# A hybrid attention layer: TensorE's order in its linear attention written out as one woven sequence, and six mask steps placed around the fifth block

## The chip, the cores and the metric

The kernel runs on one core of a Trainium2 chip. The metric is the device time of one execution in microseconds (us). The engines are TensorE (PE, with PEld for its weight loads), VectorE (DVE), ScalarE (ACT), GpSimd (POOL) and SyncE (SP); each works through its own queue in order.

## What is computed

One decoder layer on 1024 tokens of width 1024. A joint projection `proj = rmsnorm(x) @ w_in` feeds two mixers. One is sparse attention, which keeps 256 keys per query, chosen by an indexer's scores. The other is gated linear attention with 4 heads, and it is here that the change lies:

```
log_a = log_sigmoid(g_lr @ gla_gate_w2 + gla_gate_b) / 16
# per chunk: b = cumsum(log_a)
attn[t,s] = sum_d q[t,d] k[s,d] exp(b[t,d] - b[s,d])    (s <= t)
o     = attn @ v + (q * exp(b)) @ state
state = exp(b_last) * state + (k * exp(b_last - b))^T @ v
o_b   = rmsnorm(o) * silu(r_gate)
```

Both outputs are projected and added to x, and a mixture of experts follows.

## The kernel before

The tokens are 8 tiles of 128. A projection of one tile is 24 matmuls of 128x384 (`project_steps`, L275; eight pieces of the depth, with high and low halves of the weights, wh and wl), collected in one of two PSUM banks `pj`. The linear attention has two pairs of heads p and, for each, four blocks u of two tiles: `gla2(0,0)` is the first block and `gla2(1,0)` the fifth of eight. Each pair has a set of projections for queries, keys and values (`project_qkv`, copied out on ACT, L405) and one for a second head's values and the output gates (`project_vr`: ACT L410 to L414, then the swish product gv on DVE, L415).

- `gla1(p,u)` prepares a block: transposes of q and k (L635, L636), for pair 0 of the gate's 16 rows too (L646, copied to glT on ACT), the gate matmul z (L651), then a chain on ACT, DVE and POOL (scans L665, L666; products L688 to L694) to the decayed operands dd.
- `gla2(p,u)` has four levels of eight small matmuls (L711) and a fifth with four (L715), each into two of three banks `mm`, from which DVE copies under a mask into `at` (L719, L724); transposes of kd; then for each tile the outputs (L741, L744) and the state (L748, DVE L752); then squares (ACT L758), a reciprocal root and o (DVE L764). It leaves `finish`, the transposes of o (L771) and their store, to be called later.
- `search` makes passes of bisection over the indexer's scores (DVE L528 on four or six tiles, ACT L521 on two), seven in all; `make_mask` builds the mask of one tile (POOL L587, DVE L589 to L595). Both are written between the blocks. After them a flag is made (PE L811, cast on DVE L813) and loaded, and an If (L815) guards a rare repair.

Up to the If a scheduler orders PE by the order in which the code is written and by its own costs (L779 to L805). Behind the If PE's order is written by hand: `weave` takes steps from a main generator and fills each step's stated time times ROOM with projections from a second one (`gla_main` and `gla_fill`: blocks five to eight with the last vr projections of pair 1 and the first attention projections).

## Time and profile before

| | before |
|---|---|
| median of 3 runs | 1082.19 us (1080.2 to 1083.65) |
| the profiled execution | 1076.3 us, span 1074.5 us |
| mean granted clock of TensorE | 0.965 |
| PE, DVE, ACT, POOL busy | 990.3, 764.2, 674.0, 382.2 us |

The linear attention's blocks lie between about 110 and 350 us of the span; the times in the rows below count from its start. Busy time says how full an engine is, not what it waits for; that is in the waits and in the timeline, where the idle time before an instruction and what ended it stand in brackets. The granted clock is the share of full speed that TensorE was given in a stretch.

### The profile page before, as it was taken

How to read it: one execution, taken by the hardware profiler on the slowest of the kernel's cores; microseconds unless marked ns; L12 is line 12 of the kernel's file. 1: busy time of each engine (PE TensorE's matmuls, PEld its weight loads, DVE VectorE, ACT ScalarE, POOL GpSimd, SP SyncE). 2: the span in 40 equal slices, each digit the busy share in tenths (PEclk: the TensorE clock that was granted, in tenths of full speed). 3: DMA queues.
4: the chain of work that ended last, by engine and by line, in shares of the span. 5: the costliest groups of instructions: out<-in, count | busy, mean ns of one | idle time of the engine just before them, and what ended most of it. 6: DMA issues, size and time to landing. Idle time of an engine off the chain costs nothing.

```text
span 1074.5 us, 17967 instructions
## 1 busy us (share of the span) xinstructions
PE 990.3 (92%) x5839; PEld 803.9 (75%) x5839; DVE 764.2 (71%) x2037; ACT 674.0 (63%) x1662; POOL 382.2 (36%) x499
## 2 busy tenths in 40 slices
PE   7799989999998999999989999949999999999892
PEld 7789878878887988988977878836666666666561
DVE  6877898684775566767765666656887778888771
ACT  7688755365555666666755533427777777777660
POOL 4510325551413225245332201254435444443421
PEclk9899989999999999999999999968999999999996
DMA  8220202020202102012131379769999999999983
GB/s 251 81 60 1 60 1 70 11 70 21 70 11 70 38 9 65 10 51 79 58 93 48 126 255 381 292 223 286 318 317 320 326 327 324 333 316 324 341 281 46
DMA packets 83206, 170.88 MB, mean 159 GB/s; under 512 B 14856, under 2 KB 45760, under 8 KB 82976
## 3 DMA queue, kind: packets, MB, share of 16 engines
q1 hardware_dynamic: 75936, 148.01, 40.8%
q0 software_dynamic: 7168, 21.65, 9.4%
q8 instruction: 48, 0.79, 0.3%
q14 instruction: 54, 0.44, 0.1%
HBM read 148.23 MB, written 26.88 MB: 163 GB/s over the span
## 4 chain that ended last, share of the span: by engine, by line
PE 59%; DMA 14%; DVE 14%; ACT 7%; issue 3%; POOL 2%; SPq 1%; POOLq 0%; ACTq 0%; DVEq 0%
PE pj L275 19%; DMA out_dram<-y,idx 10%; PE pj L1138 8%; PE mm L1512 3%; PE po L964 3%; PE pj L1463 3%; PE pj L1464 3%; PE pj L1465 3%; PE tp L952 2%; DVE w L1386 2%; PE mm L1159 1%; PE mm L936 1%; PE tp L1473 1%; PE mm L711 1%; PE mm L935 1%
## 5 line engine op out<-in xcount | busy, mean ns | idle before, releaser
L275 PE MATMUL pj<-wh,w 128*128 128x384 f32 (+1 forms) x1152 | 322.9, 347 | 6.0 <-DVE gv L415 5.0
L275 PEld LDWEIGHTS pj<-wh,w 128*128 128x128 f32 x1152 | 211.4, 193 | 13.8 <-DVE gv L415 5.6
L1385 ACT ACTIVATE w<-w 128x512 fp32r<-128x512 f32 x320 | 192.0, 628 | 46.0 <-PE mm L1465 27.5
L1386 DVE TENSOR_TENSOR w<-w,w 128x512 fp32r<-128x512 f32 x283 | 187.2, 698 | 31.7 <-ACT w L1385 28.3
L275 PE MATMUL pj<-wl,w 128*128 128x384 f32 (+1 forms) x576 | 199.3, 346 | 1.5 <-POOL wl L263 1.1
L275 PEld LDWEIGHTS pj<-wl,w 128*128 128x128 f32 x576 | 111.8, 194 | 4.7 <-POOL wl L263 1.3
L1463 PE MATMUL pj<-w,xT 128*96 128x512 f32 x256 | 105.5, 412 | 0.6 <-ACT w L1385 0.5
L1464 PE MATMUL pj<-w,xT 128*96 128x512 f32 x256 | 101.9, 398 | 2.3 <-DVE w L1386 1.2
L1465 PE MATMUL pj<-w,xT 128*96 128x512 f32 x256 | 101.7, 397 | 0.0
L1138 PE MATMUL pj<-w,mhl 128*128 128x512 f32 x384 | 101.1, 404 | 0.0
L929 POOL TENSOR_TENSOR cb<-bt,maskb 128x256 f32<-128x256 f32 (+1 forms) x64 | 43.5, 682 | 122.1 <-DVE mx L940 103.4
L1537 POOL DMA_INDIRECT out_dram<-y,idx x30 | 52.4, 1748 | 90.0 <-ACT w L1385 53.6
L263 POOL TENSOR_TENSOR wl<-wr,wh 128x384 fp32r<-128x384 f32 x58 | 59.9, 1053 | 68.3 <-ACT wh L262 67.5
L1138 PEld LDWEIGHTS pj<-w,mhl 128*128 128x128 f32 x384 | 69.4, 189 | 12.8 <-DVE mhl L1130 0.4
L1386 POOL TENSOR_TENSOR w<-w,w 128x512 fp32r<-128x512 f32 x37 | 50.5, 1364 | 46.9 <-ACT w L1385 45.6
L1512 PE MATMUL mm<-w,hT 128*96 128x512 f32 x128 | 65.4, 592 | 0.5 <-ACT hT L1502 0.5
L943 ACT ACTIVATE z<-z,mx 128x128 f32<-128x128 f32 (+7 forms) x64 | 49.5, 774 | 22.4 <-DVE mx L940 22.0
L1463 PEld LDWEIGHTS pj<-w,xT 128*96 128x96 f32 x256 | 44.2, 173 | 15.1 <-ACT w L1385 1.3
L1465 PEld LDWEIGHTS pj<-w,xT 128*96 128x96 f32 x256 | 41.8, 163 | 18.0 <-DVE xT L1477 0.2
L1464 PEld LDWEIGHTS pj<-w,xT 128*96 128x96 f32 x256 | 41.8, 163 | 17.9 <-DVE w L1386 2.7
L1473 PEld LDWEIGHTS tp<-cf,xg 96*128 96x128 f32 x256 | 40.9, 209 | 15.8 <-issue 9.3
L1463 PE MATMUL mm<-w,hTt 128*96 128x512 f32 x64 | 50.8, 794 | 0.0
(379 smaller groups left out, 2151.7 us busy)
## 6 DMA issues: line engine op xcount, KB each, us to landing
w<-in_w_exp_gate_dram SPq DMA_DIRECT2D x64, 512.0 KB, 7.7
w<-in_w_exp_up_dram SPq DMA_DIRECT2D x64, 512.0 KB, 7.7
w<-in_w_exp_down_dram SPq DMA_DIRECT2D x64, 512.0 KB, 7.7
wr<-in_w_in_dram SPq DMA_DIRECT2D x80, 128.0 KB, 2.5
xt<-in_x_dram SPq DMA_DIRECT2D x16, 512.0 KB, 4.7
mt<-mixd SPq DMA_DIRECT2D x8, 512.0 KB, 4.3
out_dram<-xt SPq DMA_DIRECT2D x8, 512.0 KB, 3.6
h2d<-h SPq DMA_DIRECT2D x7, 528.0 KB, 5.8
```

Of the source, the lines that this page charges most:

```text
L263: (V if by[kk + k] == "V" else G).tensor_tensor(b, raw[:, k], f32(a), op=OP.subtract)
L275: T.matmul(ps[:, :width], x_, y_[k], start=(k == 0 and i == 0), stop=(k == KC - 1 and i == 2))
L943: A.activation(z[:, :L], z[:, :L], AF.Exp, bias=mn, scale=-1.0, accum_out=sums[:, i:i + 1])
L1138: T.matmul(ps, lhs[:, k % 4], w[k, c], start=(k == 0 and i == 0), stop=(k == KC - 1 and i == 2))
L1385: A.activation(a, u, AF.Copy)
L1386: (G if engine == "G" else V).tensor_tensor(b, u, f32(a), op=OP.subtract)
L1463: T.matmul(ps, x[0], y[0], start=first, stop=False)
L1464: T.matmul(ps, x[0], y[1], start=False, stop=False)
L1465: T.matmul(ps, x[1], y[0], start=False, stop=last)
L1473: T.transpose(tp[:, k, :n], x["xg"][:n, :D].rearrange("n (a p k) -> n a k p", a=2, k=4)[:, hf, k], ident[:n, :n])
L1512: T.matmul(pd[:n], hT0, parts[2 * hf], start=True, stop=False)
L1537: G.indirect_dma_start(out=out[0], out_offset=bass.IndirectOffsetOnAxis(ap=idx[:CAP, e:e + 1], axis=0), in_=y[:CAP], in_offset=None, compu ...
```

## The change

The order of PE up to the If is now written out by hand too. Two generators are woven: `first_pair` (`gla1`, `gla2`, searches and masks in their order) and `first_fill` (the vr projections of pair 0, which were issued ahead of the linear attention, then all projections of pair 1). A step that is not ready yields 0, which ends the filling for that step; the first tile of a set counts double. The fifth block and all vr projections of pair 1 now lie ahead of the If, masks 2 to 4 are written before the fifth block and 5 to 7 after it. Behind the If `gla1(1,2)` starts the main generator, which before began with a lead of 4000 ns for the filling. The last block's `finish` is called after one more step of filling and ahead of the rest of it. A block's `finish` is now called in the next block whatever its pair. The tile gq of q, k and v is split in two (gq and gw), so that v can be kept for longer (11 buffers), with two copies out of PSUM in the place of one.

```diff
@@ -72,8 +72,11 @@
 SPLIT_AT = (0, 0, 0, 0, 0, 0, 0, 1)
 OPAT = (0, 3)
 SHARE = (None, (1, 1, 1, 1, 1, 1, 0.85, 1.3), (1, 1, 1, 1, 1, 1, 0.85, 1.3), (1, 1, 1, 1, 1, 1, 1, 1.3))
-ROOM = (2.2, 2.8, 3.15, 3.3)
+ROOM = (3, 2.4, 2.4, 2.4)
+LEAD = (10000, 10000)
 OROOM = (0, 0, 0, 6000, 6000, 6000, 6000, 6000, 0)
+ROOM0 = (4, 4, 4, 4)
+MORE = 3
 LOG_FLOOR = -21.0 * 16.0
 LEVELS = (64, 32, 16, 8)
 BUCKET_START = [0, 1, 2, 3, 4, 5, 6, 7, 8, 9, 10, 11, 12, 13, 14, 15, 16, 19, 21, 24, 27, 31, 35, 40, 46, 52, 59,
@@ -237,7 +240,7 @@
     wp = p_h.enter_context(tc.tile_pool(name="wp", bufs=WBUFS, side="right"))
     hT = []
     p2 = ExitStack()
-    gqp = p2.enter_context(tc.tile_pool(name="gqp", bufs=10, side="right"))
+    gqp = p2.enter_context(tc.tile_pool(name="gqp", bufs=1, side="right"))
 
     p1 = ExitStack()
     scp = p1.enter_context(tc.tile_pool(name="scp", bufs=1, side="left"))
@@ -390,7 +393,7 @@
                         base=0, channel_multiplier=1)
 
 
-    gq, gv, pools = {}, {}, {}
+    gq, gw, gv, pools = {}, {}, {}, {}
 
     def qkv_load(p):
         c = p * P
@@ -401,8 +404,11 @@
         return load_w([(VB + 2 * c + P, P), (RG + 2 * c, 2 * P)], by=BY_VR[p])
 
     def evac_qkv(p, t, pj):
-        gq[p, t] = gqp.tile([P, 384], F32, name="gq", tag="gq", bufs=9)
-        A.activation(gq[p, t], pj[:, :384], AF.Copy, scale=rstd[:, t:t + 1])
+
+        gq[p, t] = gqp.tile([P, 256], F32, name="gq", tag="gq", bufs=NT)
+        gw[p, t] = gqp.tile([P, P], F32, name="gw", tag="gw", bufs=NT + MORE)
+        A.activation(gq[p, t], pj[:, :256], AF.Copy, scale=rstd[:, t:t + 1])
+        A.activation(gw[p, t], pj[:, 256:384], AF.Copy, scale=rstd[:, t:t + 1])
 
     def evac_vr(p, t, pj):
         g = pools["gvp"].tile([P, 384], F32, name="gv", tag="gv", bufs=NT)
@@ -458,6 +464,7 @@
                 index_operands(NT - 1)
                 yield 1000, NT - 1
         w = vr_load(0)
+        yield 0, "v"
         for t in range(NT):
             for ns in project_steps(t, w, lambda ps: evac_vr(0, t, ps)):
                 yield ns, 0
@@ -481,7 +488,7 @@
             score_sums(t)
             if t == 3:
                 relative_bias()
-        for _ in fill:
+        while next(fill)[1] != "v":
             pass
 
     p1b.close()
@@ -622,7 +629,7 @@
             room += ns
             while room > 0:
                 ns = next(fill, None)
-                if ns is None:
+                if not ns:
                     room = 0
                     break
                 room -= ns
@@ -723,8 +730,8 @@
                 else:
                     V.copy_predicated(a[:, h], gm[:, lv, None, :].to_broadcast([P, 2, P]), pav[h])
             yield 500
-            if lv == 1 and p in gla_out:
-                gla_out.pop(p)()
+            if lv == 1 and gla_out:
+                gla_out.popitem()[1]()
             if lv == 2:
                 tk = ps_tp()
                 for i in range(2):
@@ -736,7 +743,7 @@
         po = [ps[:, :2 * P].rearrange("p (i t) -> p i t", i=2) for ps in (ps_po(), ps_mm())]
         s = st_s[p]
         for i, t in enumerate(ts):
-            vals = (gq[p, t][:, 2 * P:], gv[p, t][:, :P])
+            vals = (gw[p, t], gv[p, t][:, :P])
             for h in range(2):
                 T.matmul(po[h][:, i], a[:, h, i], vals[h], start=True, stop=(t == 0))
             for h in range(2):
@@ -776,33 +783,59 @@
 
         gla_out[p] = finish
 
-    run(gla1(0, 0))
-    search(0)
-    search(1)
-    w = qkv_load(1)
-    run(gla1(0, 1))
-    for u in range(4):
-        run(gla2(0, u))
-        project_qkv(1, 2 * u, w)
-        project_qkv(1, 2 * u + 1, w)
-        if u < 2:
-            search(2 * u + 2)
-            search(2 * u + 3)
-            run(gla1(0, u + 2))
-        elif u == 2:
-            search(6)
-            search_end()
-            run(gla1(1, 0))
-    gla_out.pop(0)()
-    run(gla1(1, 1))
-    make_mask(2)
-    make_mask(3)
-    make_mask(4)
-    w = vr_load(1)
-    for t in range(4):
-        project_vr(1, t, w)
-    for t in range(5, NT):
-        make_mask(t)
+    ended = [0, 0]
+
+    def first_pair():
+        yield from gla1(0, 0)
+        yield LEAD[0]
+        search(0)
+        search(1)
+        yield from gla1(0, 1)
+        yield LEAD[1]
+        ended[1] = 2
+        for u in range(4):
+            for ns in gla2(0, u):
+                yield ns * ROOM0[u]
+            ended[0] = u + 1
+            if u < 2:
+                search(2 * u + 2)
+                search(2 * u + 3)
+                yield from gla1(0, u + 2)
+                ended[1] = u + 3
+            elif u == 2:
+                search(6)
+                search_end()
+                yield from gla1(1, 0)
+        yield from gla1(1, 1)
+        for t in range(2, 5):
+            make_mask(t)
+        for ns in gla2(1, 0):
+            yield ns * ROOM[0]
+        for t in range(5, NT):
+            make_mask(t)
+
+    def first_fill():
+
+        for ns, _ in fill0:
+            yield ns
+        w = qkv_load(1)
+        for t in range(NT):
+            while t >= MORE and ended[0] <= (t - MORE) // 2 or ended[1] <= t // 2:
+                yield 0
+            for ns in project_steps(t, w, lambda ps: evac_qkv(1, t, ps)):
+                yield ns if t else 2 * ns
+        w = vr_load(1)
+        for t in range(NT):
+            while ended[0] <= t // 2:
+                yield 0
+            for ns in project_steps(t, w, lambda ps: evac_vr(1, t, ps)):
+                yield ns if t else 2 * ns
+
+    fill0 = fill
+    with tc.manual_schedule(engines={mybir.EngineType.PE}):
+        fill = first_fill()
+        weave(first_pair(), fill)
+        run(fill)
 
 
     nb16 = const.tile([P, 1], F16, name="nb16")
@@ -893,26 +926,22 @@
                     attention_operands(*list(qk2s)[0])
                     yield 440
 
-    def gla_fill(w):
-        for t in range(4, NT):
-            yield from project_steps(t, w, lambda ps: evac_vr(1, t, ps))
-        load_bias(0, ap1)
-        yield from attention_projections(0)
-
     def gla_main():
-        yield 4000
-        for u in range(4):
+        yield from gla1(1, 2)
+        for u in range(1, 4):
             for ns in gla2(1, u):
                 yield ns * ROOM[u]
-            if u < 2:
-                yield from gla1(1, u + 2)
+            if u == 1:
+                yield from gla1(1, 3)
+        yield 5000
 
     manual = ExitStack()
     manual.enter_context(tc.manual_schedule(engines={mybir.EngineType.PE}))
-    fill = gla_fill(w)
+    load_bias(0, ap1)
+    fill = attention_projections(0)
     weave(gla_main(), fill)
+    gla_out.pop(1)()
     run(fill)
-    gla_out.pop(1)()
     p2.close()
     ap2 = p_att.enter_context(tc.tile_pool(name="ap2", bufs=1, side="left"))
     kT[1] = ap2.tile([P, 2, S], F32R, name="kT1")
```

DVE's queue under the search, before. A row is line, operation, tile written and tiles read; numbers behind names are buffers. gv_1638 is the swish product of the third tile, L719 the copies of the first level, L528 (jb) a part of a search pass, L684 and L692 operands of block (0,1).

```order
L551 TENSOR_TENSOR st_den_1814<-st_clo_1811,st_chi_1812 128x6
L553 TENSOR_TENSOR st_w_1815<-st_hi_1810,st_lo_1809 128x6
L684 COPY el_2041<-eb_2039 128x2
L415 SCALAR_TENSOR_TENSOR gv_1638<-pj_1613,rstd_70,gv_1638 128x256
L552 RECIPROCAL st_den_1814<-st_den_1814 128x6
L692 TENSOR_TENSOR eb_2039<-qk_2003,eb_2039 128x256
L554 TENSOR_TENSOR st_w_1815<-st_w_1815,st_den_1814 128x6
L719 COPY_PREDICATED at0_1841<-gm_105,mm_2055 128x2x64
L719 COPY_PREDICATED at0_1841<-gm_105,mm_2056 128x2x64
L555 SCALAR_TENSOR_TENSOR st_num_1813<-st_clo_1811,st_w_1815 128x6
L719 COPY_PREDICATED at0_1841<-gm_105,mm_2063 128x4x32
L556 TENSOR_TENSOR st_v_1807<-st_lo_1809,st_num_1813 128x6
L528 TENSOR_SCALAR jb_2217,st_c_1808<-maskb_108,st_v_1807 128x384
```

The same place now (line numbers are those of the changed file: gv L421, the pass L535, the products of block (0,0) L695 to L700); gv_1864 is the third tile's gv.

```order
L535 TENSOR_SCALAR jb_2199,st_c_1576<-maskb_108,st_v_1575 128x384
L535 TENSOR_SCALAR jb_2201,st_c_1576<-maskb_108,st_v_1575 128x512
L695 TENSOR_TENSOR dd_1646<-qk_1618,dd_1646 128x2x64
L696 TENSOR_TENSOR dd_1646<-qk_1618,dd_1646 128x2x64
L695 TENSOR_TENSOR dd_1646<-qk_1618,dd_1646 128x4x32
L696 TENSOR_TENSOR dd_1646<-qk_1618,dd_1646 128x4x32
L695 TENSOR_TENSOR dd_1646<-qk_1618,dd_1646 128x8x16
L696 TENSOR_TENSOR dd_1646<-qk_1618,dd_1646 128x8x16
L700 TENSOR_TENSOR dd_1646<-qk_1618,dd_1646 128x256
L535 TENSOR_SCALAR jb_2203,st_c_1576<-maskb_108,st_v_1575 128x640
L535 TENSOR_SCALAR jb_2205,st_c_1576<-maskb_108,st_v_1575 128x768
L421 SCALAR_TENSOR_TENSOR gv_1864<-pj_1732,rstd_70,gv_1864 128x256
```

The third tile's gv moved from ahead of a pass to behind it, and the copies of the first level from ahead of this pass to behind the next one.

PE around the flag, before (L811 is the flag, L646 the transposes of the gate's rows, L275 a projection, L651 the gate matmul, L711 a level):

```order
L811 LDWEIGHTS nb_3227
L811 MATMUL pj<-ch,nb_3227 1x1
L646 MATMUL tp<-cf,glr 16x128 x2
L275 MATMUL pj<-wh,w_323 128x384
L815 UNCONDITIONAL_BRANCH
L275 MATMUL pj<-wl,w_323 128x384
L275 MATMUL pj<-wh,w_323 128x384 x2
...
L651 MATMUL tp<-glT,w_106 128x256
L275 MATMUL pj<-wh,w_323 128x384
L275 MATMUL pj<-wh,w_356 128x384
L711 MATMUL mm<-dd 128x64 x4
```

And now (L844 the flag, L278 a projection, L718 a level):

```order
L278 MATMUL pj<-wh,w_423 128x384
L844 LDWEIGHTS nb_3465
L844 MATMUL pj<-ch,nb_3465 1x1
L278 MATMUL pj<-wh,w_133 128x384
L848 UNCONDITIONAL_BRANCH
L718 MATMUL mm<-dd 128x64 x4
L278 MATMUL pj<-wl,w_133 128x384
...
L278 MATMUL pj<-wl,w_133 128x384
L718 MATMUL mm<-dd 128x64 x4
```

Where 23 projections stood between the flag and the next block's levels, one stands there, and seven between the first two levels.

PE at the end of the last block, before (L744 the outputs, L861 the transposes of an attention tile, L771 the block's output, L935 the first scores of the attention); between L861 and L771 stand 15 projections:

```order
L744 MATMUL po<-st_s_1840,eb 128x128
L744 MATMUL mm<-st_s_1840,eb 128x128
L861 MATMUL tp<-cf,qk_4510 128x128 x4
L275 MATMUL pj<-wh,w_422 128x384
...
L275 MATMUL pj<-wh,w_423 128x384
L771 MATMUL tp<-cf,o 128x128 x4
L935 MATMUL mm<-kT_3644,qp 128x128
L936 MATMUL mm<-kT_3644,qp 128x128
```

And now (L751, L894, L778 and L964); 24 projections stand ahead of the attention's transposes and 9 behind:

```order
L751 MATMUL po<-st_s_1608,eb 128x128
L751 MATMUL mm<-st_s_1608,eb 128x128
L278 MATMUL pj<-wh,w_389 128x384
...
L278 MATMUL pj<-wh,w_423 128x384
L894 MATMUL tp<-cf,qk_4561 128x128 x4
L278 MATMUL pj<-wh,w_422 128x384
...
L278 MATMUL pj<-wh,w_423 128x384
L778 MATMUL tp<-cf,o 128x128 x4
L278 MATMUL pj<-wh,w_422 128x384
...
L278 MATMUL pj<-wh,w_423 128x384
L964 MATMUL mm<-kT_3882,qp 128x128
```

The output's transposes have 33 projections between them and the last outputs, where they had 15, and six more now stand behind them.

## Rows read from the trace of the kernel before

**Rows 1.** The page's first part (busy us, share of the span and instructions of each engine) and, of its fourth part, the chain that ended last by engine.

```profile
PE 990.3 (92%) x5839; PEld 803.9 (75%) x5839; DVE 764.2 (71%) x2037; ACT 674.0 (63%) x1662; POOL 382.2 (36%) x499
...
PE 59%; DMA 14%; DVE 14%; ACT 7%; issue 3%; POOL 2%; SPq 1%; POOLq 0%; ACTq 0%; DVEq 0%
```

**Rows 2.** Busy time by engine in the one stretch from 90 to 370 us: its length, then PE, PEld (weight loads), DVE, ACT and POOL with the number of instructions, the granted clock as a share of full speed, DMA share and GB/s.

```profile
90.00:370.00 280.00, 264.23 (x1665) 234.50 (x1664) 202.81 (x631) 164.39 (x438) 99.80 (x153) 0.97 0.15 40
```

**Rows 3.** PE's waits from 100 to 360 us: who waited for what, total us, how many times, the longest.

```profile
PE pj L275 <- DVE gv L415: 5.0, 2, 2.6
PE tp L771 <- DVE o L764: 4.9, 1, 4.9
PE mm L711 <- DVE dd L689: 2.1, 1, 2.1
PE po L741 <- DVE at L724: 1.9, 2, 1.3
PE pj L275 <- POOL wl L263: 1.1, 1, 1.1
```

**Rows 4.** Busy time by engine from 130 to 170 us, 10 us to a row, with the columns of rows 2.

```profile
130.00:140.00 10.00, 7.85 (x50) 7.31 (x48) 9.93 (x32) 7.05 (x15) 4.83 (x12) 1.00 0.00 1
140.00:150.00 10.00, 7.41 (x35) 7.07 (x35) 9.96 (x36) 5.36 (x10) 3.72 (x7) 0.66 0.01 2
150.00:160.00 10.00, 10.00 (x66) 9.36 (x64) 9.63 (x45) 5.46 (x14) 0.00 (x0) 1.00 0.00 0
160.00:170.00 10.00, 10.00 (x66) 9.06 (x65) 10.00 (x27) 6.20 (x14) 7.15 (x8) 1.00 0.48 120
```

**Rows 5.** Busy time by engine in the stretches behind the waits that end at 142.6, 218 and 346.6 us, with the same columns (the granted clock is the figure ahead of the DMA share).

```profile
142.60:146.40 3.80, 3.79 (x12) 3.79 (x13) 3.76 (x15) 2.59 (x4) 0.00 (x0) 0.50 0.01 4
...
218.00:220.00 2.00, 2.00 (x10) 1.66 (x9) 1.72 (x4) 2.00 (x4) 0.00 (x0) 0.61 0.00 0
220.00:222.00 2.00, 2.00 (x8) 2.00 (x8) 1.93 (x3) 1.95 (x3) 0.82 (x2) 0.54 0.00 0
...
346.60:349.00 2.40, 2.37 (x10) 2.23 (x11) 1.75 (x7) 0.76 (x2) 0.00 (x0) 0.50 0.49 119
349.00:351.50 2.50, 2.50 (x10) 2.40 (x9) 0.00 (x0) 0.00 (x0) 0.00 (x0) 0.50 0.31 105
```

**Rows 6.** The chain that ended last, in order of time: start, us, what ran.

```profile
142.61 6.32 PE pj L275 x24
...
154.74 4.17 PE pj L275 x24
```

**Rows 7.** ACT's timeline near 121 us: start, us, engine, line, operation, tile written and tiles read with their shapes.

```profile
120.87 0.34 ACT L410 ACTIVATE gv<-pj,rstd 128x128 f32<-128x128 f32 x1
```

**Rows 8.** ACT's timeline, one pair of search passes.

```profile
121.86 1.04 ACT L521 ACTIVATE ja<-maskb,st_v 128x896 bf16<-128x896 bf16 x1
...
123.21 1.13 ACT L521 ACTIVATE ja<-maskb,st_v 128x1024 bf16<-128x1024 bf16 x1
```

**Rows 9.** DVE's timeline: the two scans of a block, gv of the third tile, and the four sums of one search pass.

```profile
135.03 0.74 DVE L665 TENSOR_TENSOR_SCAN b<-zb 128x128 f32<-128x128 f32 x2
...
135.73 0.90 DVE L666 TENSOR_TENSOR_SCAN bc<-l 128x128 f32<-128x128 f32 x2
...
142.09 0.47 DVE L415 SCALAR_TENSOR_TENSOR gv<-pj,rstd,gv 128x256 f32<-128x256 f32 x1
...
143.81 0.61 DVE L528 TENSOR_SCALAR_CACHE_REDUCE jb<-maskb,st_v 128x384 bf16<-128x384 bf16 x1
...
144.68 0.74 DVE L528 TENSOR_SCALAR_CACHE_REDUCE jb<-maskb,st_v 128x512 bf16<-128x512 bf16 x1
...
145.75 0.87 DVE L528 TENSOR_SCALAR_CACHE_REDUCE jb<-maskb,st_v 128x640 bf16<-128x640 bf16 x1
...
146.54 1.01 DVE L528 TENSOR_SCALAR_CACHE_REDUCE jb<-maskb,st_v 128x768 bf16<-128x768 bf16 x1
```

**Rows 10.** PE's timeline around the flag (its one matmul, and the first level of a block behind it), and DVE's (the flag's cast, and the next operation with the idle time before it and what ended that).

```profile
254.34 0.16 PE L811 MATMUL pj<-ch,nb 128*1 128x1 f16 x1
...
260.10 0.66 PE L711 MATMUL mm<-dd 64*128 64x64 f32 x8
...
254.54 0.15 DVE L813 CAST flag<-pj 1x1 int32<-1x1 f32 x1 [2.98 <-PE pj L811]
258.80 0.48 DVE L415 SCALAR_TENSOR_TENSOR gv<-pj,rstd,gv 128x256 f32<-128x256 f32 x1 [4.11 <-DVEq L815]
```

**Rows 11.** PE's timeline behind the If: the projection that waited for a weight half.

```profile
290.01 0.45 PE L275 MATMUL pj<-wl,w 128*128 128x384 f32 x1 [1.13 <-POOL wl L263]
```

**Rows 12.** The last block's output: ACT's timeline (the first square of its outputs, and two weight copies with the wait before them), DVE's (the last o) and PE's (the output's transposes).

```profile
338.54 0.28 ACT L758 ACTIVATE gsq<-po 128x128 f32<-128x128 f32 x1
...
342.07 0.94 ACT L262 ACTIVATE wh<-wr 128x384 fp32r<-128x384 f32 x2 [0.59 <-DMA wr<-in_w_in_dram]
...
346.92 0.34 DVE L764 SCALAR_TENSOR_TENSOR o<-mm,ms,gv 128x128 f32<-128x128 f32 x1
...
346.63 1.16 PE L771 MATMUL tp<-cf,o 128*128 128x128 f32 x4 [4.93 <-DVE o L764]
```

## The prediction

> **What bounds the kernel now.** I read the busy times first, then the chain that ended last, then TensorE's waits, then the clock, and last the queues of the engines that TensorE waits for. TensorE (PE) is busy for 990.3 of the 1074.5 us, VectorE (DVE) for 764.2, ScalarE (ACT) for 674.0, and PE holds 59% of the chain [rows 1]. So the change is worth what it takes from PE's idle time, or adds to it. All that it moves runs between 100 and 350 us. There PE is busy for 264.23 of 280 us [rows 2], so 15.8 us are idle, and the waits name who ends them: DVE's swish gate gv (L415) 5.0 us in two waits, DVE's output o (L764) 4.9 us in one, DVE's decay operands dd (L689) 2.1, DVE's scores at (L724) 1.9, GpSimd's weight halves (L263) 1.1 [rows 3]. DVE stands behind nearly all of it, and from 130 to 170 us it is busy for 9.63 to 10.00 us of every 10 [rows 4]: there the search passes (L528) lie in the same queue as everything that PE waits for. [...] The chain shows the price: 24 projection matmuls take 4.17 us at full clock and 6.32 us behind the wait that ends at 142.61 [rows 6]. Busy time times what the clock lacks of 1 gives the loss: 3.79 x 0.50 = 1.9 us at 142.6, 2.00 x 0.39 + 2.00 x 0.46 = 1.7 at 218, 2.37 x 0.50 + 2.50 x 0.50 = 2.4 at 346.6, 6 us in all [rows 5]. So the most that any order of PE could win here is 15.8 + 6 = 22 us, or 2%. One projection matmul is 4.17 / 24 = 0.174 us; I use that price below.
>
> **What it changes nothing in.** The copy out of PSUM is split in two (gq and gw), which adds 16 instructions on ACT; the nearest row, a 128-wide copy from the same bank, is 0.34 us [rows 7], so 16 x 0.34 = 5.4 us are added to an engine that is 63% busy and ends none of the five waits above. I cost it at nothing; if ACT had no room, the swish gates behind it would come late, and these 5.4 us are the bound. The matmuls themselves are the same in number and shape. So the sum has four terms, all of them waits.
>
> **Term 1, the blocks of the first pair, up to the fifth block.** Before, the projections of values and gates (vr) for pair 0 were run between the first two transposes and the first levels, where the scheduler put them; now they are shared out among these, and 61 of them (10.6 us) stand between z of block (0,1) and the first level. That takes away the wait of the levels for dd, 2.1 us, and, as gv of tile 0 now stands ahead of the scans in DVE's queue, the first of the two waits for gv, about 2.4 us [rows 3]. Gone: 4.5 us. What is late next is read off DVE's and ACT's queues. (a) z of block (0,1) needs a copy on ACT that can come behind a pair of search passes of 1.04 and 1.13 us [rows 8]: 0 to 2.4 us with their read-outs. (b) gv of tile 2 now stands behind one search pass more, 0.61 + 0.74 + 0.87 + 1.01 = 3.2 us, but ahead of the scans of the next block, 0.74 + 0.90 = 1.6 us, which came before it at 142.09 [rows 9]: 0 to 1.6 us. (c) The levels' copies into at now stand behind a pass each. A level has 12 or 13 projections (2.1 to 2.3 us) behind it, the pass takes 3.2: 0 to 1.0 us in each of two levels. (d) At the end of block (0,2) no projection may be run, since the next tile of q, k would overwrite operands (the generator yields 0 until the block has ended). There the outputs wait for at as in the two waits of 1.9 us before [rows 3], now with no cover: 0 to 1.3 us more for each of two tiles. The new waits add up to between 0 and 8.6 us. DVE is full here, so I take two thirds, 5.7, and the term is 5.7 - 4.5 = +1.2 us. Whether the half-clock stretch behind 142.6 goes, stays or is doubled is worth 2.15 us either way [rows 6]; I leave it as it is. Ends: -6.6 and +6.3.
>
> **Term 2, the If.** The flag (L811) is a matmul on PE, its cast is on DVE, and DVE then loads it and branches. Before, the flag ran at 254.34, the cast at 254.54, and DVE's next operation started only at 258.80, after 4.11 us of its own queue [rows 10]. PE did not care: glr's transposes and 23 projections stood behind the flag. Now the flag is followed by one projection, the first level of block (1,1), seven projections, and the next level, and that one needs a PSUM bank that DVE frees only after the branch. PE has work for 0.17 + 0.66 + 1.22 = 2.1 us (a level's eight matmuls take 0.66 [rows 10]). DVE is back 258.80 - 254.34 = 4.46 us behind the flag, and then has one product and one copy to do, neither of them larger than the gv of 0.48 us in the same rows; at 0.4 each PE goes on after 5.2 us: 3.1 us idle, which is cover that was there before and is gone. Some of DVE's other work (the first operands of block (1,1)) is late by the same, and a half-clock stretch as behind the other three waits may follow: I add 1.1 us for both. Term: +4.2 us; ends +1 (DVE's return hidden under a late arrival of PE) and +6. [...]
>
> **Term 3, blocks six to eight.** These are run with the attention projections as filling, 56 of these to a block where there were 66, so the levels stand closer together. Of the five waits only the 1.1 us for GpSimd, at 290.01, lies between 255 and 341 us [rows 11]. Ends 0 and +2.5 (one more wait for at of 1.3 us in two of three blocks); I take +0.5.
>
> **Term 4, the last block's output.** Before, its transposes (L771) stood behind the attention transposes and 15 projections, and then PE waited 4.93 us for o. The chain between is on ACT and DVE: the squares start at 338.54, ACT then stood 0.59 us at a weight DMA and copied two weight tiles, and the last o starts at 346.92, while the transposes begin at 346.63 with the first ones [rows 12], so it takes 8.1 us up to the first transpose. Now 33 projections (5.7 us) stand there, 18 more, with the same attention transposes. If the chain stays as slow, 8.1 - 5.7 = 2.4 us of idle is left; without the weight copies in its way, none. I take 1.0. The half clock behind it, 2.4 us, goes with the long idle. Term: -(4.93 - 1.0) - 2.4 = -6.3; ends -7.3 and -2.5 (2.4 us idle left and the clock as before).
>
> **Sum.** 1.2 + 4.2 + 0.5 - 6.3 = -0.4 us. It is made against the profiled execution, 1076.3 us (span 1074.5). The median of the runs shown is 1082.19, with 1080.2 to 1083.65 around it; the difference carries over, so I forecast 1081.8 us, which is no difference: a measurement of this kernel tells about 0.3% (3.2 us) from no change.
>
> **The rivals.** Faster: the sharing-out really covers. Term 1 loses the 4.5 us and gets half of the new waits (4.3), DVE's return is partly under PE's arrival (term 2 +1), and term 4 gives all of its 7.3 us, -0.2 + 1 - 7.3 = -6.5, and with the half-clock stretch at 142.6 gone too -8.6: 1073.6 to 1075.7 us. For it speaks that one idle of 4.93 us and its clock are nearly half of all that is to be had and that its cover is plainly longer now; against it, that DVE has no idle time in 130 to 170 us to give. Slower: the If decides. DVE's 4.11 us now lie on PE's path, and if PE arrives at the flag with nothing queued but eight projections, all of 6 us are paid; the first blocks pay their 6.3 as well if DVE reaches each level behind a search pass, and term 4 returns only 5. 6 + 6.3 + 1 - 5 = +8.3: up to 1090.5 us, and from 3.2 us of term 1 on it is slower to be measured. For it speaks the full DVE [rows 4], against it that PE's idle can only move within that stretch as long as DVE sets its pace: what PE waits earlier, it need not wait later. That is the third: DVE paces 115 to 172 us whatever PE's order is, term 1 is zero, and the If and the last block cancel: 4.2 + 0.5 - 6.3 = -1.6, or 1080.6 us, which falls in with my forecast. [...]
>
> **How the numbers follow.** No difference (my forecast and the third rival): 0.38, from 1079 to 1085.4 us. Faster: 0.36. Slower: 0.26. The terms' ends come together rarely, so the range reaches to the two rivals' times and leaves out about a tenth on each side: 1072 to 1089 us.
>
> **What would show it.** In the profile after: the wait of the last block's transposes for o under 2.4 us, and the clock near 1 behind it (term 4); a wait of PE for at or for a level's copy of 3 us or more right behind the flag (term 2); no wait for dd, and waits for gv and z in the stretch under the search (term 1); nothing new in blocks six to eight. I am wrong if DVE is back sooner than 4 us after its cast, if PE's idle up to the fifth block is below 5 or above 13 us, or if the time of the stages behind (the attention and the experts, whose code is the same) moves by more than 1 us.

## The result

The changed kernel takes 1093.07 us (median of 5 runs, 1092.3 to 1098.4), the kernel before 1082.19 us beside it (5 runs, 1077.35 to 1086.44). The ratio is 1.0113, with a 95% interval of 1.008 to 1.0147: slower by about 12 us, which is outside the range that was forecast, 1072 to 1089 us, and above the slower rival.

The profiled execution has a span of 1090.5 us where that of before had 1074.5. Four marks on PE's timeline divide it: the first scores of the attention (L935, now L964), the last ones (L935, L964), the first expert matmul (L1463, L1492), and the last of its kind (L1512, L1541).

| stage | before, us | after, us | difference |
|---|---|---|---|
| start to the first scores | 347.44 | 353.61 | +6.2 |
| to the last scores | 271.6 | 273.4 | +1.9 |
| to the first expert matmul | 110.2 | 110.3 | +0.2 |
| to the last expert matmul | 324.9 | 333.1 | +8.2 |

The last line can't be put down to the change. An experiment below (`b_fin_new`) turned out to have the same order of PE as the kernel before, and took 335.6 us there; over all runs of this study the stage lies between 324.9 and 343.5 us. The profile of before was a short one: 1076.3 us where its median is 1082.2.

The page of the changed kernel, its first part and the busiest group of projections, beside [rows 1, 3]:

```profile
PE 995.7 (91%) x5839; PEld 806.4 (74%) x5839; DVE 758.5 (70%) x2037; ACT 673.8 (62%) x1678; POOL 385.0 (35%) x499
...
L278 PE MATMUL pj<-wh,w 128*128 128x384 f32 (+1 forms) x1152 | 326.6, 350 | 7.4 <-DVE gv L421 6.2
```

PE's waits from 90 to 370 us in the changed kernel (who waited for what, us, times, longest), beside [rows 3]:

```profile
PE pj L278 <- DVE gv L421: 6.2, 3, 2.8
PE tp L658 <- ACT glT L654: 3.0, 1, 3.0
PE mm L722 <- DVE at L726: 2.2, 2, 1.4
PE mm L718 <- DVE at L726: 2.1, 1, 2.1
PE tp L658 <- ACT qk L645: 1.6, 1, 1.6
PE tp L894 <- DVE qk L887: 1.4, 1, 1.4
PE po L748 <- DVE at L731: 1.2, 1, 1.2
```

Of the five waits of before, those for dd and for o are gone, as forecast, and those of the outputs for at (L741, now L748) and for GpSimd's weight halves are shorter. The one for gv has grown from 5.0 to 6.2 us, and five others of over 1 us have come. Each is small; the next rows show what follows them. They are stretches of the changed kernel behind three of these waits (busy time of PE, PEld, DVE, ACT, POOL, then the granted clock, DMA share, GB/s), beside [rows 5]:

```profile
220.00:227.00 7.00, 7.00 (x32) 5.14 (x33) 2.12 (x9) 2.76 (x12) 0.46 (x1) 0.52 0.00 1
227.00:239.00 12.00, 12.00 (x88) 10.24 (x87) 7.62 (x18) 6.87 (x17) 9.20 (x16) 1.00 0.47 122
...
288.30:291.30 3.00, 3.00 (x12) 2.88 (x12) 2.51 (x11) 0.00 (x0) 0.00 (x0) 0.54 0.94 247
308.30:315.30 7.00, 7.00 (x35) 5.95 (x35) 4.16 (x13) 2.08 (x5) 3.64 (x9) 0.55 0.00 0
```

Behind the waits that end at 219, 287.6 and 307.5 us PE is busy all the time at a clock of 0.52 to 0.55. Read in steps of 0.1 us from 219 to 229 us, the clock is 0.50 or 1.00 in all but two of them. From 227 us on it is 1.00 again. To price waits and clock together I add, over windows of 1 us, PE's idle time, and its busy time times what the clock lacks of 1:

| idle + lost to the clock, us | before | after |
|---|---|---|
| 90 us to the flag | 9.65 + 3.83 = 13.5 | 13.58 + 6.60 = 20.2 |
| flag to the last outputs of the last block | 1.17 + 0.00 = 1.2 | 5.03 + 5.11 = 10.1 |
| the wait for o and behind it | 4.93 + 2.46 = 7.4 | 0 |
| first 45 us of the attention (before, without that) | 0.3 | 2.29 + 0.00 = 2.3 |
| sum | 22.4 | 32.6 |

That is 10.2 us more. The two first rows do not hold the same work, since the fifth block moved from the second into the first; their sum does. By the marks the stages up to the last scores are 8.0 us longer. The 2.2 us between the two go back to the clock between 30 and 60 us, in code that the change leaves alone: it lost 4.0 us before and 1.7 after.

The same marks in a second profile of each order (`b_fin_new` and `a_mask` below) say the same: the last scores start at 619.0 and 619.6 us in the order before, and at 627.0 and 632.4 us in the changed one. So the loss lies ahead of the last scores, and is 8 to 13 us between these profiles.

### The profile page after: what moved, and what is told of

It reads as the page before. It is cut to its first block, busy times and chain, and to the rows that moved or that the text cites. A ratio compares the mean times of both kernels' runs of the same rounds, so it can differ in the third digit from the quotient of the medians.

```text
span 1090.5 us, 17975 instructions
## 1 busy us (share of the span) xinstructions
PE 995.7 (91%) x5839; PEld 806.4 (74%) x5839; DVE 758.5 (70%) x2037; ACT 673.8 (62%) x1678; POOL 385.0 (35%) x499
## 5 line engine op out<-in xcount | busy, mean ns | idle before, releaser
L278 PE MATMUL pj<-wh,w 128*128 128x384 f32 (+1 forms) x1152 | 326.6, 350 | 7.4 <-DVE gv L421 6.2
L278 PEld LDWEIGHTS pj<-wh,w 128*128 128x128 f32 x1152 | 213.3, 195 | 16.3 <-DVE gv L421 7.1
L278 PE MATMUL pj<-wl,w 128*128 128x384 f32 (+1 forms) x576 | 200.5, 348 | 0.7 <-POOL wl L266 0.7
L278 PEld LDWEIGHTS pj<-wl,w 128*128 128x128 f32 x576 | 112.5, 195 | 5.5 <-issue 1.7
L1492 PE MATMUL pj<-w,xT 128*96 128x512 f32 x256 | 105.9, 414 | 1.0 <-ACT w L1414 1.0
L1566 POOL DMA_INDIRECT out_dram<-y,idx x30 | 56.7, 1889 | 100.7 <-ACT w L1414 47.8
L266 POOL TENSOR_TENSOR wl<-wr,wh 128x384 fp32r<-128x384 f32 x58 | 59.8, 1051 | 74.2 <-ACT wh L265 74.1
L1541 PE MATMUL mm<-w,hT 128*96 128x512 f32 x128 | 65.4, 592 | 0.5 <-ACT hT L1531 0.5
L1492 PEld LDWEIGHTS pj<-w,xT 128*96 128x96 f32 x256 | 44.3, 173 | 15.4 <-ACT w L1414 1.4
L1492 PE MATMUL mm<-w,hTt 128*96 128x512 f32 x64 | 50.8, 793 | 0.0
```

Source lines behind the costliest of these rows:

```text
L266: (V if by[kk + k] == "V" else G).tensor_tensor(b, raw[:, k], f32(a), op=OP.subtract)
L278: T.matmul(ps[:, :width], x_, y_[k], start=(k == 0 and i == 0), stop=(k == KC - 1 and i == 2))
L1492: T.matmul(ps, x[0], y[0], start=first, stop=False)
L1541: T.matmul(pd[:n], hT0, parts[2 * hf], start=True, stop=False)
L1566: G.indirect_dma_start(out=out[0], out_offset=bass.IndirectOffsetOnAxis(ap=idx[:CAP, e:e + 1], axis=0), in_=y[:CAP], in_offset=None, compu ...
```

## The experiments

Names with a_ start from the changed kernel, names with b_ from the kernel before. First scores are at 353.6 us in the changed kernel and 347.4 in the kernel before; ratios are to the kernel before.

**The early output transposes, undone.**

```diff
-        yield 5000
...
-    gla_out.pop(1)()
     run(fill)
+    gla_out.pop(1)()
```

> The changed kernel with the last block's output transposes back behind all attention projections. My theory (the change loses by three uncovered waits and their half-clock stretches, and the early output transposes are a gain): the wait for o of 4.9 us comes back with about 2.4 us at half clock behind it, and the first scores of the attention start at 360 us of the span instead of 353.6. Rival (the early output brings nothing, since what stands behind it waits for the same chain): the first scores start within 1.5 us of 353.6.

Ratio 1.0104 (1.0033 to 1.0175). First scores at 359.5, as my theory had it, but not for its reason: there is no wait for o. The last block's outputs and their transposes now have 39 projections between them. The 5.9 us come from elsewhere: up to the flag this kernel has the order of the changed one and the same idle time (13.53 against 13.58 us), but lost 13.97 us to the clock, not 6.60. This part of the theory fell.

**The early output transposes alone, on the kernel before.**

```diff
+        yield 5000
...
-    run(fill)
     gla_out.pop(1)()
+    run(fill)
```

> The kernel before with this one part of the change alone: the last block's output transposes after one more step of filling and ahead of the rest. My theory: the wait of 4.9 us and its half-clock stretch go, the first scores start at 341 us instead of 347.4, and the whole kernel is 6 us faster, 0.994 of before. Rival (the time gained is given back in the attention, whose projections then wait for DVE): no difference to be measured.

Ratio 0.9976 (0.9939 to 1.0012), first scores at 348.3, the wait for o still 4.9 us. One step of 5000 ns takes some 30 projections, and only 15 were left; so the order of PE came out as before, row for row. It serves as a second profile of the kernel before. Calling the transposes sooner moves nothing by itself; what can be won hangs on how many projections are left.

**Projections held back for the end, on the kernel before.** To the edit above:

```diff
-ROOM = (2.2, 2.8, 3.15, 3.3)
+ROOM = (2.2, 2.8, 2.9, 2.7)
```

> The kernel before with the fillings of the last two blocks cut (ROOM of 2.9 and 2.7 in place of 3.15 and 3.3), so that 33 projections stand between the last outputs and their transposes in place of 15. My theory (the saving at the end comes from projections held back for it): the wait of 4.9 us and its half-clock stretch go, no new wait over 1 us in the last two blocks, first scores 5 to 7 us earlier than in the kernel before with its old filling. Rival (what is taken from the blocks comes back there as waits for at): first scores within 2 us.

Ratio 0.9986 (0.9951 to 1.0021). The wait for o is gone; the output's transposes start with no idle time before them, beside [rows 12], and only the next tile's transposes wait:

```profile
347.30 0.60 PE L771 MATMUL tp<-cf,o 128*128 128x128 f32 x4
...
350.38 0.63 PE L861 MATMUL tp<-cf,qk 128*128 128x128 f32 x4 [0.69 <-DVE qk L854]
```

From the flag to the first scores this kernel is idle for 2.37 us and loses nothing to the clock, with 1.13 idle in the first 45 us of the attention: 3.5 us. Before it was 6.10 and 0.40, with 0.32 idle and 2.06 lost to the clock in those 45 us: 8.9 us. So the saving is 5.4 us, and is due to the 33 projections. One part of my theory missed: a wait of 1.24 us for at is new, at 318 us. The first scores are still at 347.7, since this run lost 11.3 us to the clock before the flag, in code that is as before, where the other two runs of that code lost 3.8 and 6.1. In the whole time it can't be told from no difference, and of all orders that differ from the one before it is the only one that is not slower.

**The split copies alone, on the kernel before.**

```diff
-        gq[p, t] = gqp.tile([P, 384], F32, name="gq", tag="gq", bufs=9)
-        A.activation(gq[p, t], pj[:, :384], AF.Copy, scale=rstd[:, t:t + 1])
+        gq[p, t] = gqp.tile([P, 256], F32, name="gq", tag="gq", bufs=NT)
+        gw[p, t] = gqp.tile([P, P], F32, name="gw", tag="gw", bufs=NT + 3)
+        A.activation(gq[p, t], pj[:, :256], AF.Copy, scale=rstd[:, t:t + 1])
+        A.activation(gw[p, t], pj[:, 256:384], AF.Copy, scale=rstd[:, t:t + 1])
```

> The kernel before with gq split in two tiles and two copies on ACT, nothing else. My theory: 16 more ACT instructions cost nothing, the ratio is 1.000 and the first scores start at 347.4 within 1 us. Rival (ACT's queue ahead of the swish gates is on the path): first scores 2 to 5 us later.

Ratio 1.0099 (1.0064 to 1.0133), first scores at 358.5: neither theory. The order of PE ahead of the If is the scheduler's there, and with two more rows on ACT it came out otherwise: the transposes of q and k of block (1,1) behind the flag and among the levels of block (1,0), its gate matmul later still. PE then waits 3.8 us for ACT's l and 4.9 us for at near 280 and 296 us, and loses 4.5 us to the clock. What the 16 copies cost by themselves is not shown by this; in the changed kernel PE's order is written out, and no wait there is put down to them.

**Cover behind the If, first try: two tiles of vr left for the filling behind it.**

```diff
-        for t in range(NT):
+        for t in range(6):
             while ended[0] <= t // 2:
...
+    def gla_fill():
+        for t in range(6, NT):
+            yield from project_steps(t, left[0], lambda ps: evac_vr(1, t, ps))
+        load_bias(0, ap1)
+        yield from attention_projections(0)
```

> The changed kernel with the last two tiles of the vr projections of pair 1 left behind the If, so that these 48 matmuls are what fills the sixth block first. It does not move the flag's place in the order of the blocks. My theory of the wait behind the If (DVE's branch of 4.2 us lies on TensorE's path for want of cover): if the first levels of the block still stand directly behind the flag the wait of 2.1 us stays, and only what comes later changes; first scores within 2 us of 353.6. Rival (the attention projections as filling are what delays DVE behind the If): the wait and its half clock go, 3.5 us, first scores at 350.

Ratio 1.0158 (1.0084 to 1.0233). The level still stands behind the flag and still waits, 1.4 us for 2.1, with DVE away for 3.95 us: the branch is what it waits for, whatever the filling is. A new wait of 4.7 us for at came at 302 us (see the last section). The first scores are at 364.0 us, further off than either expectation: up to the flag the clock took 14.0 us in the place of 6.6, and from there to the last outputs 7.7 us are idle and 9.0 lost to the clock.

**Cover behind the If, second try: a lead.** In `gla_main`, ahead of `gla1(1, 2)`:

```diff
+        yield 4000
```

> The changed kernel with a lead of 24 projections behind the If, as before the change. My theory: the wait behind the flag (2.3 us and 1.5 us of half clock) goes, as DVE is back before the first level needs it; but 24 projections are missing at the end, where 15 are left between the last outputs and their transposes, so the wait of 4.9 us for o comes back with about 2.4 us of half clock: the saving at the end came from the projections that were held back there, not from calling the transposes sooner. First scores 3 to 4 us later than 353.6. Rival (the early call of the transposes is what saved it): no wait for o over 2 us, first scores near 350.

Ratio 1.0202 (1.0147 to 1.0257), first scores at 366.3. Both halves of the theory show. The flag's wait is gone, and the wait for o is back, 3.65 us, with 17 projections ahead of it. But the first scores are 12.7 us later than in the changed kernel, not 3 to 4. Up to the flag the clock took 13.9 us for 6.6, and behind the flag there are three new waits for at: 2.67 us at 297.5 us, then 1.28 and 2.17. PE's, ACT's and DVE's timeline around the first of them, and the wait for o:

```profile
297.55 1.11 PE L718 MATMUL mm<-dd 64*128 64x64 f32 x6 [2.67 <-DVE at L726]
...
365.50 1.16 PE L778 MATMUL tp<-cf,o 128*128 128x128 f32 x4 [3.65 <-DVE o L771]
...
295.38 0.52 ACT L265 ACTIVATE wh<-wr 128x384 fp32r<-128x384 f32 x1 [6.49 <-DMA wr<-in_w_in_dram]
295.81 0.46 ACT L878 ACTIVATE aqk<-pj,rstd 128x256 f32<-128x256 f32 x1
296.17 0.36 ACT L879 ACTIVATE va<-pj,rstd 128x128 f32<-128x128 f32 x1
296.42 0.41 ACT L881 ACTIVATE asq<-aqk 128x256 f32<-128x256 f32 x1
...
296.87 0.42 DVE L883 TENSOR_REDUCE asm<-asq 128x4 f32<-128x256 f32 x1 [6.15 <-ACT asq L881]
297.20 0.49 DVE L726 COPY_PREDICATED at<-gm,mm 128x128 f32<-128x128 uint8 x2
```

With the attention projections as lead, the first attention tile is ready to be copied out (L878) before ACT has got past a weight copy (L265), which waits 6.49 us for its DMA. DVE's sum of squares of this tile (L883) stands ahead of the level's copies (L726) in DVE's queue, and so PE waits 2.67 us for a weight DMA whose weights this level does not use.

**The same lead, filled with vr projections**, whose weights are in place: the last two edits together.

> The changed kernel with the last two tiles of the vr projections of pair 1 left behind the If and 24 of these matmuls run ahead of the first level there, as in the kernel before; their weights are in place already. My theory: no wait of TensorE behind the flag but the 0.2 us for its bank, and none for the chain over ACT's weight copies that the attention projections as a lead brought; the loss in the first 12 us behind the flag falls from 3.8 us to below 0.5. Rival (any lead only moves the wait to the next level): a wait over 1 us within 12 us of the flag.

Ratio 1.0103 (1.0068 to 1.0139), first scores at 351.8. Behind the flag PE waits 0.24 us and no more for 12 us; the first three levels follow without a wait. My theory held. What is left from flag to first scores is 4.15 us idle and 1.71 to the clock.

**Filling ahead of gla1(1,3).**

```diff
             if u == 1:
+                yield 2000
                 yield from gla1(1, 3)
```

> The changed kernel with a step of 2000 ns of filling ahead of gla1(1,3), which moves the attention tile's transposes away from in front of it. My theory (z of that block waits for ACT's copy of q and k, which stands behind ACT's and DVE's work for the attention transposes just before it): the wait of 1.6 us and the 3.5 us of half clock behind it go, first scores about 5 us earlier, at 348.5. Rival (ACT is behind there in any case): the wait stays over 1 us.

Ratio 1.0097 (1.0064 to 1.0129). The wait of 1.6 us for ACT's qk falls to 0.4 for kT, as my theory had it. One of 0.76 us for o comes back, as 29 projections stand there in the place of 33. From the flag to the first scores the time falls from 71.3 to 67.9 us, with 4.45 us idle and 1.70 to the clock for 5.03 and 5.11. The first scores themselves are at 354.3, since the flag was later by 4.1 us: the half clock behind 219 us lasted to 238 us, though the code up to there is that of the changed kernel:

```profile
219.00:227.00 8.00, 8.00 (x36) 5.85 (x36) 1.79 (x8) 3.25 (x13) 0.14 (x1) 0.50 0.00 1
227.00:238.00 11.00, 11.00 (x43) 9.58 (x44) 6.14 (x15) 6.05 (x14) 6.46 (x8) 0.50 0.44 104
```

**Block (0,2)'s end.**

```diff
-ROOM0 = (4, 4, 4, 4)
+ROOM0 = (4, 4, 2.5, 4)
```

> The changed kernel with ROOM0 of 2.5 in place of 4 for block (0,2): its 64 projections are spread over the whole block, so that seven or eight stand in each step of its end, where none stood. My theory (the end of this block, held back by the buffer rule, is one of the uncovered places): the waits of 1.4 and 1.2 us for at near 217 us go, and the half-clock stretch behind them, 3.4 us in the run after, with them, so the loss from 180 us to the flag falls from 6.7 to below 2 us and the flag runs at about 277 us instead of 282. Rival (DVE's mask work of 0.7 to 1.2 us each sets this place, whatever stands on TensorE): the same loss comes earlier in the block, the flag stays within 1.5 us.

Ratio 1.0068 (1.0034 to 1.0103). The rival held in the main: seven or eight projections now stand in each step, and PE still waits 1.99 us for at, ending at 219.15. From 180 us to the flag 6.1 us are lost where the changed kernel lost 6.7, and the flag is at 283.9, 1.6 us later, a little over the rival's bound. The rows on DVE in the changed kernel show why (L596, L597 and L602 build the mask of tile 7, L695 is a part of the next block's operands, L726 and L731 are the copies that PE waits for):

```profile
211.88 1.21 DVE L596 TENSOR_TENSOR b<-b,acc 128x1024 f32<-128x1024 f32 x1
213.13 1.23 DVE L597 MAX8 m<-b 128x8 f32<-128x1024 f32 x1
214.28 0.47 DVE L695 TENSOR_TENSOR dd<-qk,dd 128x128 f32<-128x128 f32 x1
...
215.14 0.81 DVE L695 TENSOR_TENSOR dd<-qk,dd 128x128 f32<-128x128 f32 x1
...
216.81 0.48 DVE L726 COPY_PREDICATED at<-gm,mm 128x128 f32<-128x128 uint8 x2
...
217.48 1.21 DVE L602 MATCH_REPLACE8 b<-k,b 128x1024 f32<-128x1024 f32 x1
218.60 0.77 DVE L731 COPY_PREDICATED at<-gm,mm 128x256 f32<-128x256 uint8 x2
```

**The masks' place.**

```diff
-        for t in range(2, 5):
-            make_mask(t)
         for ns in gla2(1, 0):
             yield ns * ROOM[0]
-        for t in range(5, NT):
+        for t in range(2, NT):
             make_mask(t)
```

> The changed kernel with all six masks written behind the fifth block. The queues of all five engines come out the same row for row, so the place of these lines in the code decides nothing. Each theory expects no difference from the changed kernel beyond what two runs of one program show: the waits in the same places, and the length of the half-clock stretches open; the stretch from 218 us, which was 7 us long in one run and 20 us in four others with the same code up to there, shows how often either comes.

Ratio 1.0105 (1.0043 to 1.0167): a second run of the changed kernel. Idle up to the flag 14.16 us, 9.62 lost to the clock; from there to the first scores 5.05 and 5.13. DVE works on the masks' main steps (L597, L602) from 178 to 222 us here and from 175 to 219 us in the changed kernel, wherever these lines stand: in both kernels ahead of the fifth block, none behind it.

**The vr projections of pair 0 ahead of the first blocks again.**

```diff
         w = vr_load(0)
-        yield 0, "v"
...
-        while next(fill)[1] != "v":
+        for _ in fill:
             pass
```

> The changed kernel with the vr projections of pair 0 issued ahead of the linear attention again, and not shared out among its first blocks; 192 matmuls fewer are left to fill these. My theory (VectorE paces the stretch under the search, so the order of TensorE only moves its idle time): the loss from 90 us to the flag stays within 3 us of the 20.2 us of the changed kernel, with more of it at the fourth block and the fifth, whose filling runs short. Rival (the sharing-out is what costs): the loss falls to the 13.5 us of the kernel before.

Ratio 1.0176 (1.0123 to 1.0228). Up to the flag 14.88 us idle and 11.61 to the clock, 26.5 us, where runs of the changed kernel's order have 20 to 28. Up to 180 us it lost 10.2 us, of them 2.10 for dd, and behind that 16.3, with one wait of 4.0 us for at. So my theory holds for the idle time, which moved and did not fall; the bound of 3 us on the sum was missed against the profile of the changed kernel, for the clock.

**All covers together** (lead of vr projections, filling ahead of gla1(1,3), ROOM0 of 2.5; the masks are written as in `a_mask`):

> The changed kernel with that lead, with filling ahead of gla1(1,3), and with block (0,2)'s filling spread by ROOM0 of 2.5. My theory: behind the flag no wait over 1 us is left up to the first scores, as in the kernel before, and the output's transposes do not wait; the waits under the search and for the masks stay. The loss from the flag to the first scores falls from 10.2 to below 2 us, and the whole is about 5 to 8 us below the changed kernel, near or above the kernel before. Rival (the tighter blocks behind the If wait whatever leads them): a loss of over 5 us there.

Ratio 1.0104 (1.0038 to 1.017). From the flag to the first scores 3.97 us idle and none to the clock, for 10.1; not the 2 us forecast, since 1.70 us for the state and 1.94 for at remained. First scores at 345.4, the earliest of all, but in a run with no half clock from 180 us to the flag. The transposes of an attention tile then wait 3.23 us at 350.6. In the whole time it is not shown to be better than the changed kernel. The same holds of `a_z` and `a_cover_lead`: their profiles save 4 us between the flag and the first scores, this one 6, and the intervals of their ratios are too wide to show that or to rule it out.

## Why the prediction was wrong

What all runs of one order have in common is the idle time; what differs between them is the clock. Five runs have the changed kernel's order up to the fifth block (after, `a_mask`, `a_fin_old`, `a_z`, `a_lead`), three that of before (before, `b_fin_new`, `b_fin_room`). Means of 90 us to the flag:

| | idle, us | lost to the clock, us |
|---|---|---|
| changed, 5 runs | 13.2 to 14.2, mean 13.7 | 6.6, 9.6, 14.0, 14.2, 13.9, mean 11.7 |
| before, 3 runs | 8.9 to 10.0, mean 9.5 | 3.8, 6.1, 11.3, mean 7.1 |

The idle time differs by more than its scatter, and all of the difference lies under the search: from 90 to 180 us it is 10.3 to 11.0 us in the five and 5.8 to 7.2 in the three, from 180 us to the flag 2.8 to 3.3 and 2.5 to 4.1. The ranges of the clock's loss overlap, so its difference is not shown in the same way.

- **Term 1** (+1.2 us) failed most: idle +4.1 and, as far as these means go, clock +4.6, so +8.7 us. PE's waits under the search in the changed kernel, and ACT's and DVE's rows behind two of them (L658 is the gate matmul z of block (0,1), L528 ACT's search pass, L654 the copy that z needs):

```profile
125.36 0.44 PE L278 MATMUL pj<-wh,w 128*128 128x384 f32 x1 [1.43 <-DVE gv L421]
133.06 0.69 PE L658 MATMUL tp<-glT,w 16*128 16x256 f32 x2 [2.96 <-ACT glT L654]
142.02 0.44 PE L278 MATMUL pj<-wh,w 128*128 128x384 f32 x1 [1.98 <-DVE gv L421]
155.78 0.69 PE L278 MATMUL pj<-wh,w 128*128 128x384 f32 x1 [2.78 <-DVE gv L421]
...
131.13 1.04 ACT L528 ACTIVATE ja<-maskb,st_v 128x896 bf16<-128x896 bf16 x1 [3.77 <-DVE st_v L563]
132.65 0.36 ACT L654 ACTIVATE glT<-tp 16x256 f32<-16x256 f32 x1
...
153.49 0.49 DVE L695 TENSOR_TENSOR dd<-qk,dd 128x128 f32<-128x128 f32 x1
155.25 0.47 DVE L421 SCALAR_TENSOR_TENSOR gv<-pj,rstd,gv 128x256 f32<-128x256 f32 x1
```

The wait for dd went, but it was worth less than the 2.1 us of one profile: two others of the order before have 0.58 and 0.56 (`b_fin_new`, `b_fin_room`). The first wait for gv, which was to go with 2.4 us, only shrank, to 1.43. Of the new ones (c) and (d) stayed small: 0.38 us for a level, and 2.64 at the end of block (0,2), where 1.92 were before. The second wait for gv, (b), did not grow: 1.98 us for 2.59. The loss came from two places. Part (a), the wait of z, was 2.96 us, above its bound of 2.4: I had priced ACT's passes, but ACT first stood 3.77 us for DVE's next search value, with the pass and the copy queued behind it. And a third wait for gv, 2.78 us, was not in the sum at all: the fifth tile's gv stands behind the next block's seven products (L695 and those after it) and half a search pass. PE's four waits shown have the same length to 0.02 us in `a_mask`. And I left the clock as it was.
- **Term 2** (+4.2 us): the mechanism was right. DVE stood for 4.16 us behind the cast, where [rows 10] have 4.11 and `a_cover` 3.95. What takes the time is not shown. PE waited at the second level:

```profile
282.31 0.16 PE L844 MATMUL pj<-ch,nb 128*1 128x1 f16 x1
...
287.59 0.66 PE L718 MATMUL mm<-dd 64*128 64x64 f32 x6 [2.06 <-DVE at L726]
...
282.51 0.14 DVE L846 CAST flag<-pj 1x1 int32<-1x1 f32 x1 [0.73 <-PE pj L844]
286.82 0.50 DVE L701 TENSOR_TENSOR en<-qk,en 128x256 f32<-128x256 f32 x1 [4.16 <-DVEq L848]
```

It cost 0.24 + 2.06 us idle, not 3.1, and about 1.4 behind it at half clock, 3.7 us in all. `a_lead` and `a_cover_lead`, in which this wait is gone, show that it is the cover which decides; the other filling of `a_cover` did not remove it.
- **Term 3** (+0.5 us, ends 0 and +2.5) failed too: 10.1 us from the flag on, less 3.7 for the If, less the 1.2 of before, is +5.2 us. The largest part is not a wait for at, which I had priced, but one that I had not seen: ACT's copy of q and k stands behind the copies of an attention tile, whose transposes the denser filling put right ahead of gla1(1,3). It is 1.59 us, and 3.2 at half clock (the row from 308.30 us above); `a_z`, which moves these transposes, takes 1.2 us of the one and all of the other away. ACT's and PE's rows:

```profile
306.58 0.38 ACT L911 ACTIVATE kT<-tp 128x256 fp32r<-128x256 f32 x1 [0.58 <-DVE qp L909]
306.86 0.59 ACT L645 ACTIVATE qk<-tp 128x512 f32<-128x512 f32 x1
...
307.50 0.69 PE L658 MATMUL tp<-pos,w 16*128 16x256 f32 x2 [1.59 <-ACT qk L645]
```

- **Term 4** (-6.3 us) was nearly right. The wait of 4.93 us and the half clock behind it went, 7.4 us, but 2.0 us come back right behind the first scores, where the attention's transposes wait for DVE's qk, a wait that I had not foreseen: -5.4 us. It is the number of projections held back (ROOM) that pays, as I had argued from 33 against 15, and not the earlier call.

The four terms as measured, 8.7 + 3.7 + 5.2 - 5.4, give +12.2 us, and the ratio of 1.0113 is 12.2 us. That they meet so closely is luck, as the clock in the first term comes from five and three runs that scatter by several us; the marks up to the last scores, 8 to 13 us, are the firmer account. The slower rival came nearest (the first blocks and the If pay, the end gives back 5); it had 0.26. It had 6 us for the If, where 3.7 were paid, and 1 for the blocks behind it, where 5.2 were. The third rival, that DVE sets the pace and term 1 is zero, fell: idle time up to the flag is up by 4 us. Of the signs of being wrong that I had set, PE's idle up to the fifth block came, above 13 us. The one on the stages behind was badly chosen: it allowed 1 us, and the expert stage differs by 10.7 us between two profiles of the order before.

Open: why the half clock behind 219 us lasted 7 us in two of the five runs of the same code and 20 in the other three, and whether the expert stage is longer by any of it; its times with the changed orders (330.7 to 343.5 us) and with the old ones (324.9 to 336.1) overlap.

## What to carry to other kernels

When an order is changed on the engine that bounds the kernel, list what stands behind every place where a slower engine is away (a branch, a search pass, a run of mask steps), and give each place cover whose own inputs, weights too, are already there. Price a short wait with the half-clock stretch that follows it, from the runs' own rows: here it cost nearly as much again as the wait (in the changed order 11.7 us for 13.7 us idle up to the flag, as means, and 5.11 for 5.03 from there to the last outputs). Take the size of a wait from more than one profile: the one for dd was 2.1 us in one and 0.6 in two others. And code that a scheduler places need not move with its lines, as the masks here did not, while a change that seems local (one copy split in two) can reorder what stands around it.

## What the runs showed that I had not expected

The same DVE product took four times as long, 1.08 us for 0.28, while GpSimd worked on weight halves. In `a_cover`, DVE's L695 and GpSimd's L266:

```profile
295.25 0.29 DVE L695 TENSOR_TENSOR dd<-qk,dd 128x128 f32<-128x128 f32 x1 [0.79 <-ACT dd L687]
...
295.66 1.13 DVE L695 TENSOR_TENSOR dd<-qk,dd 128x128 f32<-128x128 f32 x1
...
298.74 1.08 DVE L696 TENSOR_TENSOR dd<-qk,dd 128x128 f32<-128x128 f32 x1
...
300.74 0.28 DVE L696 TENSOR_TENSOR dd<-qk,dd 128x128 f32<-128x128 f32 x1
...
295.63 5.03 POOL L266 TENSOR_TENSOR wl<-wr,wh 128x384 fp32r<-128x384 f32 x5 [1.08 <-ACT wh L265]
```

0.28 us before and after, 1.07 to 1.13 us inside the 5.03 us of GpSimd's five subtractions. Five products took 5 us in the place of 1.4, each about as long as one of GpSimd's (5.03 / 5), and PE waited 4.68 us for the copies behind them. The changed kernel and the kernel before have 56 such products each. Of the 8 and 14 that overlap a TENSOR_TENSOR of GpSimd in time, 6 and 12 take over 0.4 us (0.43 to 1.11); of the 48 and 42 others one each does, with 0.91 us. What the two engines share there is not shown. In `b_split` four products take 1.08 or 1.09 us each from 290.5 us on, ahead of the wait of 4.9 us there.
